# Two layers of a hybrid decoder trunk: a closing product after the last small run, and later norm transposes

## The chip, the core and the metric

The kernel runs as one program on one core of a Trainium2 chip. The metric is device time in microseconds of one execution. Three timed runs of the kernel before gave 2418.55, 2419.78 and 2422.97 us; the median, 2419.78 us, is the time that the prediction speaks of.

## The reference, cut to what matters

Each of the two layers does this, for 256 tokens and a width of 2048:

```python
u = rms_norm(x, norm_w) * (1.0 + scale) + shift
proj = jnp.dot(u, w_in)              # fq fk fv fg dq dk dv iq ... dg sz sxbc mg
y_fox = fox_attention(fq, fk, fv, log_f) * silu(fg)
y_dsa = dsa_attention(dq, dk, dv, iq, ik, iw) * silu(dg)
xbc = silu(causal_depthwise_conv(sxbc, conv_w, conv_b))
y = (ssd_scan(xs, dt, a, b, c) + d_skip * xs) * silu(sz)
y_ssd = rms_norm(y.reshape(B, S, 4, 512), ssd_norm)     # four groups of 512 channels
merged = g0 * dot(y_fox, w_o_fox) + g1 * dot(y_dsa, w_o_dsa) + g2 * dot(y_ssd, w_o_ssd)
x = x + gate * jnp.dot(merged, w_out)
```

The change lies in the state-space branch: in the norm of `y` over each of its four groups, and in what follows the last of them.

## The kernel before, in words

Every weight matrix streams from HBM in pieces of 128x1024 (`raw`). ScalarE casts a piece into a rounded upper half `wh` (L188), VectorE subtracts to get the lower half `wl` (L189), and TensorE multiplies three times for one product: upper by upper, lower by upper, upper by lower. One piece is called a half here. There are two loops over pieces. `tok_half` (L200 to L202) writes token-major banks, 12 matmuls of 512 columns a piece. `feat` (L233 to L235) writes feature-major banks, 24 matmuls of 256 columns a piece, and each of those 24 loads its own 128x128 weights (PEld, the weight load, in the rows).

The order of TensorE and SyncE is written out by hand: the instructions stand as the program issues them. After each piece the program calls `tick`, and a tick lets each of three lanes of side jobs take one step. The side jobs are generators: `g_qk`, `g_heads`, `g_xs`, `g_ssd`, `g_norm` and so on; they hold the small products (transposes against `ident`, attention and scan products) that go between the big runs. `yield from self.wait(n)` lets a job sleep for n ticks, so the `LAG_...` numbers of L63 and L64 say how many pieces later a job's next small products come. A job's lane is strictly in turn.

The state-space branch goes over four groups, g = 0 to 3. For each, `ssd_conv` runs six `feat` blocks of two pieces each through the convolution, `ssd_rest` runs eight `tok_half` pieces for the gate `sz`, and the scan job `g_ssd` issues two runs of small products, each of one 512-column product (L1022, L1025) and eight products of 64 columns (L1032) for the two token halves. Then `g_norm` forms the norm: VectorE and ScalarE multiply `y` by the gate, square, take the reciprocal root and scale `y` (L1047 to L1054); the job sleeps `LAG_NORM` ticks; TensorE transposes `y` in eight 128x128 blocks (L1059); ScalarE and VectorE split the result into `ysh` and `ysl` (L1064, L1065). With a lag of 7 the transposes of groups 0 to 2 come in the middle of the next group's convolution blocks, and those of group 3 in the middle of `gate_y("dg")` (16 pieces).

After group 3 no small product is left in the layer. What follows on TensorE, called the tail here, is one unbroken run of 4752 `feat` matmuls: the rest of `dg`, the three branch outputs with their merge gates, and the output projection. Layer 0's tail ends at the norm of layer 1 (L383), layer 1's at the end of the program.

Small products write banks of the pool `mx` (four buffers, `pbank`), big ones banks of `mm` (four buffers).

Of the kernel before, what the change touches and what calls it, by code (L numbers as in the profile page):

```python
# [60 lines left out]
AHEAD, EARLY = 1, (1,)  # L61

LAG_RMS, LAG_SM, LAG_PV, LAG_SSD = (6, 6), (3, 3), (1, 1), 3  # L63
LAG_NORM, LAG_SMALL, LAG_TOPK, LAG_DQ = (7, 7), (8, 8), (6, 6), (7, 7)  # L64
PER_TICK = 2


# [4 lines left out]
class Net:  # L72
# [968 lines left out]
    def g_norm(self, l, g, gates, y, sp, S):  # L1041

        nc, par = self.nc, self.pr[l]
        ss = self.st([P, 2], "yss")
        for c in range(2):
            t = gates[c]
            nc.vector.tensor_mul(y[:, c, :], y[:, c, :], t)  # L1047
            nc.scalar.activation(t, y[:, c, :], AF.Square, accum_out=ss[:, c:c + 1])
        rs = self.st([P, 2], "yrs")
        self.rsqrt(rs, ss, 1.0 / 2048, EPS, "ny")  # L1050
        rh = self.st([P, 2], "yrh")
        nc.vector.tensor_scalar(rh, rs, 0.5, None, op0=OP.mult)
        for c in range(2):
            nc.vector.tensor_scalar(y[:, c, :], y[:, c, :], rh[:, c:c + 1], None, op0=OP.mult)  # L1054
        yield from self.wait(LAG_NORM[self.l])
        banks = [self.pbank() for _ in range(2)]
        for i in range(4):
            for c in range(2):
                nc.tensor.transpose(banks[i // 2][:, i % 2 * SEQ + c * P:i % 2 * SEQ + c * P + P], y[:, c, i * P:i * P + P], self.ident)  # L1059
        for i in range(4):  # L1060
            f = 4 * g + i
            pt = banks[i // 2][:, i % 2 * SEQ:i % 2 * SEQ + SEQ]
            col = par[:, COLS["ssd_norm"].start + f:COLS["ssd_norm"].start + f + 1]
            nc.scalar.activation(S.ysh[:, f, :], pt, AF.Copy, scale=col)  # L1064
            nc.vector.scalar_tensor_tensor(S.ysl[:, f, :], pt, col, S.ysh.bitcast(F32)[:, f, :], op0=OP.mult, op1=OP.subtract)  # L1065
        yield
# [67 lines left out]
```

## Time and profile before

| what | value |
|---|---|
| median of three timed runs | 2419.78 us |
| the profiled execution's own time | 2399.32 us |
| its span, first to last instruction | 2397.4 us |
| PE busy | 2353.6 us, 98% |
| DVE busy | 1740.4 us, 73% |
| ACT busy | 1198.1 us, 50% |
| mean granted TensorE clock | 0.997 |

The profiled execution was 20.46 us shorter than the median of the timed ones. PE is busy nearly throughout, and matmuls overlap in the records, so busy time does not tell how fast TensorE works. What tells it is the distance from one matmul's start to the next, or the number of matmuls in a stretch: `x4414` behind a busy time is that number, with the two that had begun before the stretch among them.

### The profile page before, as it was taken

The page shows a single profiled execution, that of the slowest core. Times are in us where ns is not written, and L with a number is a line of the kernel's source. Part 1 is how long each engine was busy: PE and PEld are TensorE (multiplying, and loading weights), DVE is VectorE, ACT ScalarE, POOL GpSimd, SP SyncE. Part 2 cuts the span into 40 slices and gives each one's busy share as a digit, 9 for nine tenths or more (in the row PEclk, how much of TensorE's full clock was granted, in tenths as well). Part 3 has the DMA queues.
Part 4 walks back from the last instruction along what each step waited for, and adds up shares of the span by engine and source line. Part 5 has one row for each costly group of instructions (what it writes and reads, how often), then busy time and mean ns, then how long its engine had stood idle before and what let it go on. Part 6 is the DMA issues. An engine that isn't in the chain of part 4 may idle for free.

```text
span 2397.4 us, 43544 instructions
## 1 busy us (share of the span) xinstructions
PE 2353.6 (98%) x17192; PEld 2196.6 (92%) x17192; DVE 1740.4 (73%) x3105; ACT 1198.1 (50%) x1916; POOL 3.5 (0%) x19
## 2 busy tenths in 40 slices
PE   6999999999999999999999999999999999999999
PEld 4778889989899999999978877999999999999999
DVE  8899979778986677777765668777787655566554
ACT  3535666756454444444445555566564444444442
POOL 0000000000000000000000000000000000000000
PEclk9999999999999999999999999999999999999999
DMA  9998434567778888888855544555666666666564
GB/s 333 337 324 307 158 124 145 192 203 243 236 263 272 275 272 273 274 272 288 300 167 185 185 131 147 179 178 192 185 217 211 223 221 228 223 223 212 186 220 141
DMA packets 149919, 536.23 MB, mean 224 GB/s; under 512 B 16913, under 2 KB 17489, under 8 KB 149713
## 3 DMA queue, kind: packets, MB, share of 16 engines
q1 hardware_dynamic: 142274, 516.61, 64.9%
q10 hardware_dynamic: 7440, 16.85, 2.2%
q8 instruction: 134, 2.20, 0.4%
q14 instruction: 71, 0.58, 0.1%
HBM read 529.13 MB, written 4.26 MB: 222 GB/s over the span
## 4 chain that ended last, share of the span: by engine, by line
PE 91%; DVE 6%; ACT 1%; DMA 1%; issue 1%; SPq 0%; DVEq 0%
PE pm L233 20%; PE pm L234 20%; PE pm L235 20%; PE pm L200 8%; PE pm L202 8%; PE pm L201 8%; DVE raw L249 2%; DVE wl L189 2%; PE px L1032 1%; PE px L496 1%; DMA dec<-rows 1%; PE px L630 1%; ACT wh L188 0%; PE px L622 0%; PE held L202 0%
## 5 line engine op out<-in xcount | busy, mean ns | idle before, releaser
L188 ACT CAST wh<-raw 128x1024 fp32r<-128x1024 f32 x788 | 826.7, 1051 | 954.2 <-PE pm L234 494.8
L189 DVE TENSOR_TENSOR wl<-raw,wh 128x1024 fp32r<-128x1024 f32 x788 | 961.5, 1221 | 410.1 <-PE pm L235 176.7
L233 PE MATMUL pm<-uh,wh 128*128 128x256 f32 x2848 | 798.1, 280 | 0.0
L235 PE MATMUL pm<-uh,wl 128*128 128x256 f32 x2848 | 791.5, 278 | 0.2 <-DVE wl L189 0.2
L234 PE MATMUL pm<-ul,wh 128*128 128x256 f32 x2848 | 791.3, 278 | 0.0
L233 PEld LDWEIGHTS pm<-uh,wh 128*128 128x128 f32 x2848 | 538.9, 189 | 2.2 <-issue 2.0
L234 PEld LDWEIGHTS pm<-ul,wh 128*128 128x128 f32 x2848 | 535.1, 188 | 0.2
L235 PEld LDWEIGHTS pm<-uh,wl 128*128 128x128 f32 x2848 | 534.6, 188 | 0.4 <-DVE wl L189 0.4
L202 PE MATMUL pm<-wl,uh 128*128 128x512 f32 x896 | 351.8, 393 | 8.5 <-DVE wl L189 8.5
L200 PE MATMUL pm<-wh,uh 128*128 128x512 f32 x896 | 355.7, 397 | 1.1 <-ACT uh L399 1.1
L201 PE MATMUL pm<-wh,ul 128*128 128x512 f32 x896 | 350.5, 391 | 0.0
L249 DVE SCALAR_TENSOR_TENSOR raw<-raw,crep 128x1024 f32<-128x1024 f32 x192 | 232.9, 1217 | 0.0
L202 PEld LDWEIGHTS pm<-wl,uh 128*128 128x128 f32 x896 | 169.1, 189 | 47.4 <-DVE wl L189 11.7
L200 PEld LDWEIGHTS pm<-wh,uh 128*128 128x128 f32 x896 | 169.3, 189 | 37.7 <-issue 2.7
L201 PEld LDWEIGHTS pm<-wh,ul 128*128 128x128 f32 x896 | 169.3, 189 | 34.2 <-DVE ul L400 0.2
L235 PE MATMUL pm<-yh,wl 128*128 128x256 f32 x512 | 142.6, 279 | 0.0
L233 PE MATMUL pm<-yh,wh 128*128 128x256 f32 x512 | 142.6, 279 | 0.0
L234 PE MATMUL pm<-yl,wh 128*128 128x256 f32 x512 | 142.6, 279 | 0.0
L235 PE MATMUL pm<-ysh,wl 128*128 128x256 f32 x512 | 142.6, 279 | 0.0
L234 PE MATMUL pm<-ml,wh 128*128 128x256 f32 x512 | 142.6, 279 | 0.0
L233 PE MATMUL pm<-ysh,wh 128*128 128x256 f32 x512 | 142.6, 278 | 0.0
L234 PE MATMUL pm<-ysl,wh 128*128 128x256 f32 x512 | 142.6, 278 | 0.0
(313 smaller groups left out, 2787.2 us busy)
## 6 DMA issues: line engine op xcount, KB each, us to landing
raw<-w_ts SPq DMA_DIRECT2D x352, 512.0 KB, 4.2
raw<-w_tm SPq DMA_DIRECT2D x240, 512.0 KB, 3.6
raw<-w_ada SPq DMA_DIRECT2D x192, 512.0 KB, 4.6
raw<-w_od SPq DMA_DIRECT2D x192, 512.0 KB, 4.3
dec<-rows ACTq DMA_DIRECT2D x32, 256.0 KB, 4.2
raw<-w_sm SPq DMA_DIRECT2D x4, 512.0 KB, 4.7
xr<-xT ACTq DMA_DIRECT2D x4, 512.0 KB, 7.4
x<-xn ACTq DMA_DIRECT2D x4, 512.0 KB, 4.6
```

Source lines behind the costliest of these rows:

```text
L188: self.nc.scalar.copy(h, src)
L189: return self.nc.vector.tensor_sub(l, src, h.bitcast(F32))
L200: mm(ps, lhsT=ah, rhs=bh, start=start, stop=False)
L201: mm(ps, lhsT=al, rhs=bh, start=False, stop=False)
L202: mm(ps, lhsT=ah, rhs=bl, start=False, stop=stop)
L233: mm(ps, lhsT=h[:, c], rhs=ah[:, k, :], start=k == 0, stop=False)
L234: mm(ps, lhsT=h[:, c], rhs=al[:, k, :], start=False, stop=False)
L235: mm(ps, lhsT=l[:, c], rhs=ah[:, k, :], start=False, stop=k == nk - 1)
L249: self.in_turn(nc.vector.scalar_tensor_tensor(r, r, 0.5, self.crep[:, n % 2 * 1024:n % 2 * 1024 + 1024], op0=OP.mult, op1=OP.mult, accum_o ...
L496: nc.tensor.transpose(ps[:, j * SEQ + th * P:j * SEQ + th * P + P], t[:, th, c0 + j * P:c0 + j * P + P], self.ident)
L630: nc.tensor.matmul(po[:, :SEQ], lhsT=v[:, 0], rhs=pT[:, :SEQ], start=True, stop=False)
L1032: nc.tensor.matmul(pd[:, c * 256 + o % 256:c * 256 + o % 256 + 64], lhsT=decs[k][:, i, c, :], rhs=xd[:, c, o:o + 64], start=True, stop=True)
```

## The change

Two edits. `LAG_NORM` goes from 7 to 9 in both layers, and behind the transposes of group 3 a matmul is issued whose result nobody reads: `ones` by 64 columns of `ones`, f32, into a fresh bank of `mx`.

```diff
-LAG_NORM, LAG_SMALL, LAG_TOPK, LAG_DQ = (7, 7), (8, 8), (6, 6), (7, 7)
+LAG_NORM, LAG_SMALL, LAG_TOPK, LAG_DQ = (9, 9), (8, 8), (6, 6), (7, 7)
 ...
         for i in range(4):
             for c in range(2):
                 nc.tensor.transpose(banks[i // 2][:, i % 2 * SEQ + c * P:i % 2 * SEQ + c * P + P], y[:, c, i * P:i * P + P], self.ident)
+        if g == 3:
+
+            nc.tensor.matmul(self.pbank("idle")[:, :64], lhsT=self.ones, rhs=self.ones[:, :64], start=True, stop=True)
         for i in range(4):
             f = 4 * g + i
```

On TensorE nothing else changes place: without the eight transposes of each group and the two new matmuls, its order is the same. On PE, in layer 0, where group 1's convolution runs, this goes out (`pm` is a big bank, `px` a small one, `uh` and `ul` the halves of the layer's input):

```order
 L234 MATMUL pm<-ul,wh 128x256
 L235 MATMUL pm<-uh,wl 128x256
-L1059 MATMUL px<-ident,y 128x128 x8
 L233 MATMUL pm<-uh,wh 128x256
 L234 MATMUL pm<-ul,wh 128x256
```

and two pieces further on, where the convolution's last piece ends and the gate's first `tok_half` begins, also on PE, this comes in:

```order
 L234 MATMUL pm<-ul,wh 128x256
 L235 MATMUL pm<-uh,wl 128x256
+L1059 MATMUL px<-ident,y 128x128 x8
 L200 MATMUL pm<-wh,uh 128x512
 L201 MATMUL pm<-wh,ul 128x512
```

So group 0's transposes moved past 48 `feat` matmuls and the run of L984, L987 and L991 between them; groups 1 and 2, and layer 1, move alike. The start of layer 1's tail on PE before:

```order
L234 MATMUL pm<-ul,wh 128x256
L235 MATMUL pm<-uh,wl 128x256
L1059 MATMUL px<-ident,y 128x128 x8
L233 MATMUL pm<-uh,wh 128x256
L234 MATMUL pm<-ul,wh 128x256
```

and now:

```order
L234 MATMUL pm<-ul,wh 128x256
L235 MATMUL pm<-uh,wl 128x256
L1059 MATMUL px<-ident,y 128x128 x8
L1062 MATMUL idle<-ones 128x64
L233 MATMUL pm<-uh,wh 128x256
L234 MATMUL pm<-ul,wh 128x256
```

The transposes stand 48 matmuls later, inside `dg` as before, and a product of 64 columns now stands between them and the tail; layer 0's tail starts alike. On ACT and DVE the instructions are the same in number; L1064 and L1065 (L1067 and L1068 in the changed file) follow their transposes by the same two pieces. No DMA changes place on SP.

## Rows read from the trace of the kernel before

**Rows 1.** The page: TensorE's busy time, and the granted clock in 40 slices.

```profile
PE 2353.6 (98%) x17192; PEld 2196.6 (92%) x17192; DVE 1740.4 (73%) x3105; ACT 1198.1 (50%) x1916; POOL 3.5 (0%) x19
...
PEclk9999999999999999999999999999999999999999
```

**Rows 2.** Busy time and instructions by stretch: layer 0's tail twice, layer 1's once.

```profile
core 0: us, PE busy (x) PEld busy (x) DVE busy (x) ACT busy (x) POOL busy (x), PEclk, DMA share, GB/s
668.00:695.00 27.00, 27.00 (x232) 27.00 (x231) 23.21 (x37) 15.94 (x22) 0.00 (x0) 1.00 0.71 228
700.00:1200.00 500.00, 500.00 (x4414) 500.00 (x4414) 357.88 (x514) 221.70 (x261) 0.00 (x0) 1.00 0.83 279
1840.00:2340.00 500.00, 500.00 (x4247) 500.00 (x4247) 289.54 (x360) 215.02 (x248) 0.00 (x0) 1.00 0.67 217
```

**Rows 3.** Instructions in order of time: start, duration (us); PE where layer 1's tail begins.

```profile
1833.43 1.03 PE L1059 MATMUL px<-ident,y 128*128 128x128 f32 x8
1834.22 0.36 PE L233 MATMUL pm<-uh,wh 128*128 128x256 f32 x1
```

**Rows 4.** In order of time: PE in layer 0's tail, around 696 us.

```profile
695.91 0.28 PE L234 MATMUL pm<-ul,wh 128*128 128x256 f32 x1
696.03 0.30 PE L235 MATMUL pm<-uh,wl 128*128 128x256 f32 x1
696.17 0.28 PE L233 MATMUL pm<-uh,wh 128*128 128x256 f32 x1
```

**Rows 5.** In order of time: a run of 64-column products, and the 48 matmuls behind it.

```profile
443.76 1.90 PE L1032 MATMUL px<-xd,dec 128*128 128x64 f32 x16
445.47 0.36 PE L233 MATMUL pm<-uh,wh 128*128 128x256 f32 x1
...
451.00 0.59 PE L1025 MATMUL px<-xe,CT 128*128 128x512 f32 x1
```

**Rows 6.** By stretch, columns as in Rows 2: two of the eight long runs behind 64-column products.

```profile
455.00:475.00 20.00, 20.00 (x179) 20.00 (x178) 17.52 (x38) 14.73 (x29) 0.00 (x0) 1.00 0.55 179
...
1813.00:1833.00 20.00, 20.00 (x179) 20.00 (x178) 17.02 (x34) 9.46 (x14) 0.00 (x0) 1.00 0.57 192
```

**Rows 7.** In order of time: eight transposes, the 24 matmuls behind them, twice.

```profile
539.83 0.98 PE L1059 MATMUL px<-ident,y 128*128 128x128 f32 x7 [1.91 <-DVE y L1054]
540.57 0.37 PE L233 MATMUL pm<-uh,wh 128*128 128x256 f32 x1
...
543.39 0.27 PE L984 MATMUL px<-ident,BT 128*128 128x128 f32 x1
...
1771.21 1.03 PE L1059 MATMUL px<-ident,y 128*128 128x128 f32 x8
1772.01 0.36 PE L233 MATMUL pm<-uh,wh 128*128 128x256 f32 x1
...
1774.92 0.27 PE L984 MATMUL px<-ident,BT 128*128 128x128 f32 x1
```

**Rows 8.** Who waited for whom on PE, whole program: us in total, times, longest.

```profile
PE px L1059 <- DVE y L1054: 3.9, 2, 2.0
```

**Rows 9.** In order of time: the two waiting transposes, and the scaling of `y`.

```profile
537.64 0.27 PE L1059 MATMUL px<-ident,y 128*128 128x128 f32 x1
...
539.29 0.47 DVE L1054 TENSOR_SCALAR y<-y,yrh 128x512 f32<-128x512 f32 x1
...
602.19 0.33 PE L1059 MATMUL px<-ident,y 128*128 128x128 f32 x1
604.50 0.98 PE L1059 MATMUL px<-ident,y 128*128 128x128 f32 x7 [1.98 <-DVE y L1054]
605.23 0.36 PE L233 MATMUL pm<-uh,wh 128*128 128x256 f32 x1
```

**Rows 10.** In order of time: transposes ahead of a `tok_half` piece.

```profile
1787.19 0.47 PE L200 MATMUL pm<-wh,uh 128*128 128x512 f32 x1
1787.51 0.39 PE L201 MATMUL pm<-wh,ul 128*128 128x512 f32 x1
```

## The prediction

> **What bounds the kernel now.** I read the page first: TensorE (PE) is busy for 98% of the span, at a granted clock of nine tenths or more in every slice [rows 1]. So waits can give little, and the question is how fast the matmuls follow each other. For that I read the table by stretches, since it counts instructions. In the two tails, where the same `feat` matmul of 256 columns runs without a break, the counts differ [rows 2]. Layer 0 from 700 to 1200 us has 4414 matmuls; without the two that had begun before, that is 500 / 4412 = 113.3 ns from start to start. Layer 1 from 1840 to 2340 us has 4247, that is 500 / 4245 = 117.8 ns. The clock is 1.00 (2.4 GHz) in both, the instructions are the same, and layer 0 moves more by DMA (279 GB/s against 217), so neither the clock nor the memory explains the slower one. From 668 to 695 us layer 0's tail was slow as well: 27 / 230 = 117.4 ns. There are two paces, fast and slow, 4.46 ns apart, and a tail keeps the one it has: layer 1's stayed slow for 4752 matmuls, layer 0's went over at 696 us, at one matmul that came 0.14 us before the next and not 0.12 [rows 4], and then stayed fast.
>
> Next I looked at what stands ahead of each `feat` run in order of time. Behind the sixteen runs that end on 64-column products the pace is fast. One short one: 48 matmuls from 445.47 to 451.00, of which the first takes 0.09 more than its pace, so (5.53 - 0.09) / 48 = 113 ns [rows 5]; there are eight of these. Of the eight long ones, every stretch of 20 us holds 179 starts (20 / 177 = 113.0 ns; the slow pace would give 172) [rows 6], of which the first and the last stand there. Behind the eight runs of L1059, which are transposes alone, the pace is slow seven times: both tails [rows 2, 3] and five of six short stretches, which take 2.91 us for 24 matmuls where the one fast one takes 2.82 [rows 7]. So what ends a run of small products goes with the pace behind it, and the one before a tail decides over 4752 matmuls.
>
> Last, the waits. PE waits twice for the scaled `y` at L1059, 1.91 and 1.98 us [rows 7, 8, 9], both in layer 0.
>
> **The closing product.** It puts a 64-column f32 product between the eight transposes and each tail, the same kind of ending as the sixteen of L1032: a full 128x128 load of f32 weights, 64 columns, then L233. If it works as they do, both tails run fast from the start.
>
> Layer 1: 4752 x 4.46 ns = 21.2 us less.
>
> Layer 0, in the profiled execution: only the stretch from 667 to 696 us was slow, some 29 us, or 29 / 0.1178 = 246 matmuls, so 246 x 4.46 ns = 1.1 us less. The profiled execution took 2399.32 us, and the timed ones 2419.78: 20.46 more. Had layer 0's tail stayed slow to its end, (4752 - 246) x 4.46 ns = 20.1 us would have been added. I take this as the reason for the gap: nothing broke the slow pace in the timed runs. So against the timed median layer 0 gives 21.2 us, too.
>
> Between the ends, nothing and 42.4 us for both tails, I take 42.4. It is nearest to the rows: sixteen of sixteen endings on 64 columns were fast. What keeps it from being sure is that each of those runs had eight such products at its end, never a single one behind transposes.
>
> The product itself: the eight of an L1032 run stand in the trace as sixteen matmuls, two for each f32 product, and take (445.47 - 443.76) / 8 = 0.21 us each [rows 5]. Below, nothing can be gained by issuing it. Above, its bank was last used four banks earlier, by the product of L1025, which VectorE read before it formed this group's norm; so it should not wait; my upper end is the 0.80 us that eight transposes take without a wait [rows 7], should it stop the flow. I take 0.2 each, or +0.4 us for both.
>
> **The later transposes.** In the two places with a wait, PE takes from the first transpose to the next L233 540.57 - 537.64 = 2.93 us and 605.23 - 602.19 = 3.04 us, where it takes 0.80 without a wait (1771.21 to 1772.01) [rows 7, 9]. That is 2.13 + 2.24 = 4.4 us lost. In the new place PE comes 48 matmuls and a small run later, over 5.4 us. `y` was ready at 539.29 + 0.47 = 539.76 [rows 9], 2.1 us after PE came. So 3.3 us are to spare, and I cost the wait at nothing left: -4.4 us. If VectorE fell behind by more than that, PE would wait again, with the gate's first `tok_half` queued behind; the ends are -4.4 and 0. No other wait of PE stands between 430 and 1200 us in the waits, so I see nothing that is late next. ScalarE's and VectorE's split of the transposes (L1064, L1065) moves by the same two pieces, to where the gate begins; it is read only in the third branch's projections, far behind.
>
> The other costs are small. The five short slow stretches go (their 24 matmuls now run on from the convolution): 5 x 0.09 = -0.5 us. In place of that a `tok_half` starts six times behind transposes, with a first step of 0.32 us [rows 10] against 0.23 within a piece (half a slow step for 512 columns, 2 x 113 ns): +0.5 us. Sum 0.
>
> **Sum.** Against the profiled execution: 2399.32 - 21.2 - 1.1 + 0.4 - 4.4 = 2373.0 us. Against the median of the timed runs: 2419.78 - 42.4 + 0.4 - 4.4 = 2373.4 us. The two agree, as they should if the gap between them was layer 0's pace. I forecast 2373 us.
>
> **Rivals.**
>
> *The closing product sets nothing.* For it: one fast stretch behind transposes alone [rows 7] and the change of pace in mid-run [rows 4] show that the last product is not the whole story; it may be the rhythm of eight equal products that brings the fast pace. Against it: sixteen of sixteen. Then only the waits go: 2419.78 - 4.4 + 0.4 = 2415.8 us, a gain of 0.17%.
> The Trainium skill, in "TensorE: Matmul & The Clock Gate" (section "Back-to-back issue gap"), speaks for this rival: the spacing is set by the load and the matmul, pipelined through a window of 64 instructions, with N / 2.4 + 2.5 ns for one matmul alone. By that an unread product has no effect 64 instructions later, and the estimate for 256 columns is 109 ns whatever came before. The trace does not agree: two paces, 113.3 and 117.8 ns, each held over more than 4000 matmuls.
>
> *One tail only.* Either the product works in one layer, or the 20 us between the profiled and the timed executions have another cause and layer 0's tail was fast in both. Both give one tail's worth: 2419.78 - 21.2 - 4.4 = about 2394 us. For the second reading: the trace shows one execution alone, and its layer 0 did run fast. Against it: 20.1 us worked out from the pace and 20.46 measured.
>
> *The closing product brings the slow pace.* This is the other side. If layer 0's tail is fast in the timed runs, and the new product's weight load puts the tail into the slow rhythm and nothing breaks it at 696 us, layer 0 pays 20.1 us and layer 1 stays as it is: 2419.78 + 20.1 - 4.0 = 2436 us. It decides as soon as more than 4.0 us / 4.46 ns = 900 matmuls that ran fast become slow. Against it stand the same sixteen endings, and the 20.46 us.
>
> **How the numbers follow.** Chances: the forecast 0.70, one tail 0.13, nothing set 0.13, the slow side 0.04. For the forecast alone, with the waits' gain between 2 and 5 us and a few tenths for the products, the range is 2369 to 2377. The range for 8 in 10 takes in the one-tail case: 2367 to 2397 us, which leaves out the last two with 0.17. A measurement of this kernel can tell about 0.2%, or 4.8 us, from no change. The first two cases are faster by more. The third, at 4.0 us, lies just inside, and I split it: 0.05 faster, 0.07 same, 0.01 slower. Together 0.88 faster, 0.07 same, 0.05 slower.
>
> **What the profile of the changed kernel would show.** Right: both tails with 4414 or so matmuls in 500 us (113.3 ns), from their first microseconds on; no wait for `y` at L1059; the profiled execution within a few us of the timed ones. Wrong: a tail with 4247 in 500 us though a 64-column product stands ahead of it, which would refute that the ending sets the pace; or a wait at L1059 or L1062, in which case the lag has only moved it. If both tails are fast in the profile and the time is nonetheless near 2394 us, the 20.46 us were not layer 0's pace.

## The result and the profile after

The changed kernel takes 2393.52 us (median of 2391.74, 2393.52 and 2394.08), the kernel before 2419.78. The ratio is 0.9887, with a 95% interval of 0.9865 to 0.9910. That is 26.3 us less where 46.4 were forecast. The profiled execution of after took 2393.52 us itself, 5.8 less than the profiled one of before (2399.32). So the two kernels differ by 5.8 us when one looks at profiles and by 26.3 us when one looks at medians. Most of what follows is about that difference.

First the page of after, its busy times and the granted clock, which answer to [rows 1]:

```profile
PE 2352.6 (98%) x17196; PEld 2195.8 (92%) x17196; DVE 1740.6 (73%) x3105; ACT 1198.0 (50%) x1916; POOL 3.5 (0%) x19
...
PEclk9999999999999999999999999999999999999999
```

The page hardly tells the kernels apart: four matmuls more (two f32 products of two matmuls each) and 1.0 us of busy time less. As before, it is the count of matmuls in a stretch that says something. Here are the stretches of after that answer to [rows 2], columns as there:

```profile
670.00:690.00 20.00, 20.00 (x172) 20.00 (x172) 17.08 (x26) 12.73 (x16) 0.00 (x0) 1.00 0.66 209
700.00:1200.00 500.00, 500.00 (x4414) 500.00 (x4413) 356.76 (x510) 221.79 (x262) 0.00 (x0) 1.00 0.82 278
1840.00:2340.00 500.00, 500.00 (x4247) 500.00 (x4247) 289.24 (x359) 215.25 (x247) 0.00 (x0) 1.00 0.67 217
```

Layer 0's tail begins slow (172 in 20 us; the fast pace gives 179), and is fast from 700 us on. Layer 1's tail has 4247 matmuls in 500 us, the same number as before. Both tails now stand behind a 64-column product, and both begin slow all the same. This is what the prediction named as its refutation.

TensorE in order of time (start, duration, operation) shows why the waits went and where layer 0's pace changed:

```profile
544.17 1.03 PE L1059 MATMUL px<-ident,y 128*128 128x128 f32 x8
544.96 0.48 PE L200 MATMUL pm<-wh,uh 128*128 128x512 f32 x1
...
691.38 0.31 PE L235 MATMUL pm<-uh,wl 128*128 128x256 f32 x1
691.53 0.28 PE L233 MATMUL pm<-uh,wh 128*128 128x256 f32 x1
...
1833.20 1.03 PE L1059 MATMUL px<-ident,y 128*128 128x128 f32 x8
1834.07 0.33 PE L1062 MATMUL idle<-ones 128*128 128x64 f32 x2
1834.21 0.36 PE L233 MATMUL pm<-uh,wh 128*128 128x256 f32 x1
1834.42 0.28 PE L234 MATMUL pm<-ul,wh 128*128 128x256 f32 x1
```

The moved transposes of 544 us run through in 0.79 us without a wait, where they took 2.93 before [rows 7, 9]; no row of TensorE's waits names L1059 any more [rows 8]. At 691.38 stands the counterpart of [rows 4]: one matmul that comes 0.15 us before the next and not 0.12, at the third matmul of a group, the first to read `wl`. The closing product itself costs what was worked out: from the first transpose to L233 it is 1834.21 - 1833.20 = 1.01 us, where [rows 3] have 0.79, so 0.22 more.

What holds that one matmul back can be read on VectorE and on the weight loads (PEld), in order of time in the same execution:

```profile
684.01 2.35 DVE L189 TENSOR_TENSOR yl<-yf,yh 128x1024 fp32r<-128x1024 f32 x2
686.28 2.35 DVE L189 TENSOR_TENSOR yl<-yd,yh 128x1024 fp32r<-128x1024 f32 x2
...
690.03 2.35 DVE L189 TENSOR_TENSOR wl<-raw,wh 128x1024 fp32r<-128x1024 f32 x2
...
691.15 0.19 PEld L234 LDWEIGHTS pm<-ul,wh 128*128 128x128 f32 x1
691.30 0.19 PEld L235 LDWEIGHTS pm<-uh,wl 128*128 128x128 f32 x1
```

Four splits of the branch outputs (`yl`) stand ahead of the weight's. The first of the two `wl` is ready at about 690.03 + 1.22 = 691.25 us, and the load that reads it as weights starts at 691.30, 0.15 us behind the load before it, where the slow pace has 0.12. So TensorE waits some 0.03 us, too little for a row in the view of waits, and goes on at the other pace. The trace of before has the same wait at [rows 4].

### The profile page after: what moved, and what is told of

Read it like the earlier page. It is cut to its first block, busy times and chain, and to the rows that moved or that the text cites. A ratio compares the mean times of both kernels' runs of the same rounds, so it can differ in the third digit from the quotient of the medians.

```text
span 2391.7 us, 43556 instructions
## 1 busy us (share of the span) xinstructions
PE 2352.6 (98%) x17196; PEld 2195.8 (92%) x17196; DVE 1740.6 (73%) x3105; ACT 1198.0 (50%) x1916; POOL 3.5 (0%) x19
## 4 chain that ended last, share of the span: by engine, by line
PE 93%; DVE 6%; issue 1%; ACT 0%; DMA 0%; SPq 0%; DVEq 0%; ACTq 0%
PE pm L233 21%; PE pm L235 21%; PE pm L234 21%; PE pm L200 8%; PE pm L202 8%; PE pm L201 8%; DVE wl L189 2%; DVE raw L249 2%; PE px L1032 1%; PE px L496 1%; PE px L630 1%; PE held L202 0%; PE px L622 0%; PE held L200 0%; PE held L201 0%
## 5 line engine op out<-in xcount | busy, mean ns | idle before, releaser
L233 PE MATMUL pm<-uh,wh 128*128 128x256 f32 x2848 | 797.3, 280 | 0.0
L233 PEld LDWEIGHTS pm<-uh,wh 128*128 128x128 f32 x2848 | 534.9, 188 | 2.2 <-issue 2.0
L233 PE MATMUL pm<-yh,wh 128*128 128x256 f32 x512 | 142.6, 279 | 0.0
L233 PE MATMUL pm<-ysh,wh 128*128 128x256 f32 x512 | 142.6, 278 | 0.0
L233 PE MATMUL pm<-mh,wh 128*128 128x256 f32 x512 | 142.6, 278 | 0.0
```

Of the source, the lines that this page charges most:

```text
L233: mm(ps, lhsT=h[:, c], rhs=ah[:, k, :], start=k == 0, stop=False)
```

## Experiments

The theory after the result: the 64-column product does nothing to the pace, the later transposes are worth some 6 us, and the other 20 us are layer 0's tail, which was slow to its end in the three timed runs of before and turns fast at the wait for `wl` in other executions. Rivals: the rhythm of eight equal products is what makes the fast pace; or the edit does work, but its product is too short; or the 20 us are a difference between executions that has nothing to do with the pace. In each of three sets of runs before was timed again on the same chip; its times fell in two groups, 2397.7 to 2404.4 and 2418.2 to 2425.0 us. Where a ratio mixes these, I compare with the nearest kernel of the same set.

**Before again, and the two edits apart.** e1 is before, unchanged. e2 has only

```diff
-LAG_NORM, LAG_SMALL, LAG_TOPK, LAG_DQ = (7, 7), (8, 8), (6, 6), (7, 7)
+LAG_NORM, LAG_SMALL, LAG_TOPK, LAG_DQ = (9, 9), (8, 8), (6, 6), (7, 7)
```

and e3 has only

```diff
+        if g == 3:
+            nc.tensor.matmul(self.pbank("idle")[:, :64], lhsT=self.ones, rhs=self.ones[:, :64], start=True, stop=True)
```

> The kernel before, unchanged, to see an execution at its timed level. Theory A (layer 0's tail stayed slow in the timed runs, and the profiled execution at 2399.32 us is one in which a short wait for wl broke the slow pace): executions fall into two groups, about 2399 and 2419 us; in a profile at 2419 layer 0's tail has about 4247 matmuls in 500 us throughout, in one at 2399 about 4414. Rival B (the 20 us have another cause): a profiled execution at 2419 us still shows 4414 matmuls in 500 us in layer 0, or executions spread evenly.

> Only the norm lag of 9; no closing product. Theory A (the product sets no pace; the gain is the two waits and layer 0's tail breaking into the fast pace more reliably because of where the tail now begins): 2393 us, as with both edits, both tails slow at their start. Theory C (the product is what lets layer 0 break): layer 0's tail slow to its end in the timed runs, 2419.8 - 4.4 = 2415 us.

> Only the closing product, norm lag of 7. Theory A: the waits at L1059 are back, so 4 us above both edits if layer 0's tail breaks (2398 us), or as before (2420 us) if it does not; both tails start slow. Theory C (the product lets layer 0 break): 2398 us. The prediction's step, that the product makes both tails fast from the start, would give 2378 us.

Measured: e1 2399.89 us (2397.74 to 2403.88, ten runs), e2 2393.98 (2391.83 to 2397.21, seven), e3 2400.26 (2398.68 to 2403.95, ten); before beside them 2402.26, with one of 24 runs in the upper group. So the lag alone gives 5.9 us against e1, and 7.0 by its ratio to the runs of before beside it (0.9971, 0.9960 to 0.9982). The product alone gives +0.4, which can't be told from zero: e1 and the runs beside it are one kernel and lie 2.4 us apart. In e3 both tails begin slow, as in after:

```profile
670.00:690.00 20.00, 20.00 (x172) 20.00 (x171) 15.99 (x29) 9.89 (x14) 0.00 (x0) 1.00 0.80 264
1840.00:2340.00 500.00, 500.00 (x4248) 500.00 (x4247) 288.95 (x361) 215.35 (x248) 0.00 (x0) 1.00 0.66 217
```

The view of waits gives for e1 (us in total, times, longest), where [rows 8] had two waits:

```profile
PE px L1059 <- DVE y L1054: 4.7, 3, 2.0
```

There is a third, small one in this execution (0.85 us), so 4.4 us was a low reading of what the lag can give.

**Is the product too short?** e4 is after with 256 columns in place of 64, e7 with 128:

```diff
-nc.tensor.matmul(self.pbank("idle")[:, :64], lhsT=self.ones, rhs=self.ones[:, :64], start=True, stop=True)
+nc.tensor.matmul(self.pbank("idle")[:, :SEQ], lhsT=self.ones, rhs=self.tri, start=True, stop=True)   # e4
+nc.tensor.matmul(self.pbank("idle")[:, :P], lhsT=self.ones, rhs=self.ones, start=True, stop=True)    # e7
```

> Both edits, but the unread closing product is 256 columns wide (ones by tri, f32) and not 64. In the trace of before all runs that end on f32 products of 256 columns (L682, L721) are followed by the fast pace. Theory D (what counts is that TensorE streams a product longer than a weight load, so that the load of the first feat matmul stands behind it): both tails fast from the start, 2393.5 - 20.9 - 1.0 + 0.3 = 2372 us. Theory A (no closing product sets the pace, only a wait does): 2393 to 2394 us, layer 1's tail slow.

> Both edits, with an unread closing product of 128 columns. Theory D (the product has to outlast the weight load ahead of the tail): the two matmuls of a 128-column product are about as long as a load, so it lies at the edge; L631 with 128 columns is followed by the fast pace in the trace of before, but behind L630 with 256. Fast in both tails gives 2372 us and would mean that any f32 product over 64 columns does; slow gives 2393.6 us and puts the edge between 128 and 256.

e4 took 2374.41 us (2372.70 to 2376.66, four runs), 19.6 below e2 of the same set; its ratio to before is 0.9888 (0.9872 to 0.9905). By stretches, e4:

```profile
700.00:1200.00 500.00, 500.00 (x4414) 500.00 (x4414) 356.93 (x510) 221.93 (x261) 0.00 (x0) 1.00 0.81 278
1840.00:1860.00 20.00, 20.00 (x179) 20.00 (x178) 17.52 (x24) 12.39 (x15) 0.00 (x0) 1.00 0.66 199
1870.00:2360.00 490.00, 490.00 (x4326) 490.00 (x4326) 284.83 (x352) 213.03 (x241) 0.00 (x0) 1.00 0.68 221
```

And TensorE in order of time where layer 1's tail begins, to be held against after's rows at 1833 us:

```profile
1833.59 1.03 PE L1059 MATMUL px<-ident,y 128*128 128x128 f32 x8
1834.46 0.60 PE L1062 MATMUL idle<-tri,ones 128*128 128x256 f32 x2
1834.71 0.47 PE L233 MATMUL pm<-uh,wh 128*128 128x256 f32 x1
1835.02 0.28 PE L234 MATMUL pm<-ul,wh 128*128 128x256 f32 x1
```

Layer 1's tail has 179 in its first 20 us and 4326 in 490 us: 490 / 4324 = 113.3 ns, the fast pace. The transposes ahead, the operands of the tail and the code around it are the same as in after; only the product's columns differ (and the operand they are read from).

Three of e7's four runs took 2372.01, 2372.77 and 2373.30 us, and the profiled one 2391.68. Its stretches tell why:

```profile
668.00:688.00 20.00, 20.00 (x178) 20.00 (x178) 17.61 (x27) 12.75 (x17) 0.00 (x0) 1.00 0.65 215
700.00:1200.00 500.00, 500.00 (x4248) 500.00 (x4247) 346.00 (x494) 213.90 (x251) 0.00 (x0) 1.00 0.80 269
1850.00:2350.00 500.00, 500.00 (x4415) 500.00 (x4414) 299.61 (x374) 224.03 (x259) 0.00 (x0) 1.00 0.69 226
```

Both tails begin fast, so 128 columns do as well. But layer 0's turned slow in this execution, at the same wait for `wl` where after's turned fast:

```profile
688.91 0.28 PE L234 MATMUL pm<-ul,wh 128*128 128x256 f32 x1
689.27 0.39 PE L235 MATMUL pm<-uh,wl 128*128 128x256 f32 x1
```

The two starts are 0.36 us apart here, so TensorE waits 0.25 us; the tail came fast and is earlier at this place. e4 and e12 have the same 0.36 and stay fast. One more place can be compared, in every profiled execution: 74 matmuls into a run of 192 in layer 1 (1505.95 us in after), which is fast until there, the starts stand 0.44 us apart, so TensorE waits 0.33 us for `wl`. Behind it ten of the fourteen stay fast and four turn slow (e1, e4, e6, e7). By stretch, after and then e4:

```profile
1508.00:1518.00 10.00, 10.00 (x91) 10.00 (x90) 6.62 (x10) 4.30 (x5) 0.00 (x0) 1.00 0.78 272
1508.00:1518.00 10.00, 10.00 (x87) 10.00 (x87) 6.22 (x10) 3.91 (x5) 0.00 (x0) 1.00 0.81 264
```

So a wait at the fast pace can leave that pace or end it. At the slow pace a wait was followed by the fast one in all ten places that were profiled (layer 0 of before, after, e1, e2, e3, e5, e6, e10 and e11, layer 1 of e10); a wait with the slow pace on both sides was not seen.

**Or the rhythm of eight?** e6 is after with eight 64-column products, as an L1032 run has them:

```diff
+            ib = self.pbank("idle")
+            for i in range(8):
+                nc.tensor.matmul(ib[:, i * 64:i * 64 + 64], lhsT=self.ones, rhs=self.ones[:, :64], start=True, stop=True)
```

> Both edits, but eight unread 64-column products (1.7 us a layer) and not one. Theory E (the rhythm of several equal f32 products is what the sixteen L1032 runs have and a single product lacks): both tails fast, 2393.5 - 21.9 + 3.0 = 2375 us. Theory D (what counts is a last product longer than a load of weights, as in the one of 256 columns): both tails start slow, 2393.5 + 3.0 = 2396.5 us.

The ten runs fell in two groups, five at 2397.5 to 2398.3 us and five at 2416.2 to 2418.8. In the profiled one, of the lower group, TensorE's rows read like those of [rows 5], but with transposes ahead of them:

```profile
1836.42 1.03 PE L1059 MATMUL px<-ident,y 128*128 128x128 f32 x8
1837.29 1.90 PE L1064 MATMUL idle<-ones 128*128 128x64 f32 x16
1838.99 0.36 PE L233 MATMUL pm<-uh,wh 128*128 128x256 f32 x1
```

The next 20 us of this execution by stretch:

```profile
1840.00:1860.00 20.00, 20.00 (x172) 20.00 (x171) 14.60 (x20) 11.92 (x14) 0.00 (x0) 1.00 0.53 175
```

172 is the slow pace, so the rhythm theory falls. A run that looks the same, down to the 0.36 us of the first L233, is followed by the fast pace in the sixteen places of before and by the slow one here.

**Take layer 0's wait away.** e8 is before, with the split of `yd` in layer 0 moved from the tail's first weight to its later ones, so that VectorE has `wl` ready earlier:

```diff
-                    self.split(yh[:, a:a + 4], yl[:, a:a + 4], src[:, a:a + 4])
+                    if l or not n:
+                        self.split(yh[:, a:a + 4], yl[:, a:a + 4], src[:, a:a + 4])
...
+                if l == 0 and br == 0 and c in (8, 12):
+                    a = c % 8
+                    with self.first():
+                        self.split(yhl[1][0][:, a:a + 4], yhl[1][1][:, a:a + 4], yd[:, a:a + 4])
```

> The kernel before, but layer 0 splits yd into yh and yl eight and twelve channel blocks into the first branch and not ahead of it, so that VectorE is 2.3 us earlier with the wl that TensorE waits for at 696 us. Theory A (that wait of a tenth of a us is what makes layer 0's tail fast): the wait is gone and with it the fast pace; layer 0's tail has about 4247 matmuls in 500 us and the time is 2399.9 + 20 = 2420 us, the level of the three timed runs of before. Rival (layer 0's tail turns fast for another reason): 4414 in 500 us and 2400 us, or 2399.7 without the wait.

It took 2422.34 us (2418.14 to 2424.30): all ten runs lie in the upper group, while before beside it had 15 of 25 in the lower and 10 in the upper. Layer 0's tail by stretch:

```profile
700.00:1200.00 500.00, 500.00 (x4248) 500.00 (x4247) 347.35 (x493) 213.07 (x250) 0.00 (x0) 1.00 0.80 269
```

Here `wl` is ready at 697.60 + 1.22 = 698.82 us and read 2.74 us later:

```profile
697.60 1.22 DVE L189 TENSOR_TENSOR wl<-raw,wh 128x1024 fp32r<-128x1024 f32 x1
```

With no wait nothing ends the slow pace. The upper group is thus what a slow layer 0 costs: 22.5 us above the lower one's median in this set (2399.88), where 20.1 were worked out from the pace. That before's upper runs have the same cause is an inference from this: no execution of before in the upper group was profiled, so it isn't known either whether the wait leaves layer 0 slow there or, at 0.03 us, does not come at all.

**Make such a wait in layer 1.** e5 and e10 are after with two, and three, further writes of the last `yl` piece on VectorE ahead of `wl`:

```diff
+                if l == 1 and n == 1:
+                    for _ in range(2):          # e10: 3
+                        nc.vector.tensor_sub(yl[:, 4:8], src[:, 4:8], yh[:, 4:8].bitcast(F32))
```

> Both edits, and in layer 1 VectorE computes the last piece of yl twice more (2.3 us of work with the same result), ahead of a wl that TensorE found ready only 1.6 us before its use. TensorE then has to wait some 0.7 us for wl about 24 us into layer 1's tail, as it waits shortly in layer 0's. Theory A (a wait of TensorE inside a slow run is what turns it fast): layer 1's tail slow until there, then 4414 matmuls in 500 us; 2393.5 - (4704 - 240) x 4.46 ns + 0.7 = 2374 us, faster by doing more. Rival (only what stands ahead of a run, or which layer it is, sets its pace): layer 1's tail slow to its end, 2393.5 + 0.7 = 2394 us.

> Both edits with the 64-column product, and in layer 1 three more repeats of the last piece of yl on VectorE, since two left wl 0.70 us before its use and made no wait. With three, wl ends some 0.45 us after TensorE comes for it, 26 us into layer 1's tail, which is slow there. Theory A2 (a wait deals the pace anew): layer 1's tail fast from there in some or all executions, 2393.5 + 0.5 - 20.5 = 2373 to 2374 us where it is; a mix of 2374 and 2394 would show the dealing. Rival (layer 1's pace is not open to a wait): 2394 us throughout.

e5 took 2395.52 us (2391.89 to 2397.77) and tested nothing: two repeats left the nearest `wl` ready 0.70 us early, TensorE did not wait, and the tail stayed slow. e10 took 2373.61, 2375.65 and 2376.10 us, and once 2397.26 (median 2375.87, ratio to before 0.9844, 0.9788 to 0.9900). In the profiled run of 2375.65 us, by stretch, ahead of the wait and behind it:

```profile
1840.00:1860.00 20.00, 20.00 (x172) 20.00 (x171) 16.44 (x23) 12.14 (x15) 0.00 (x0) 1.00 0.59 183
1870.00:2360.00 490.00, 490.00 (x4326) 490.00 (x4326) 285.80 (x352) 213.80 (x243) 0.00 (x0) 1.00 0.68 223
```

And between them TensorE in order of time:

```profile
1864.53 0.28 PE L234 MATMUL pm<-ul,wh 128*128 128x256 f32 x1
1864.65 0.33 PE L235 MATMUL pm<-uh,wl 128*128 128x256 f32 x1
1864.82 0.28 PE L233 MATMUL pm<-uh,wh 128*128 128x256 f32 x1
```

The wait is shorter than expected (0.05 us and not 0.45) and comes one piece later, 28.6 us into the tail. Some 3.5 us of useless work on VectorE, and this wait on the engine that bounds the kernel, make it about 20 us faster. This is the clearest evidence that a wait sets the pace: the rest of the kernel is after's, and e5 has two of the three repeats, no wait, and a slow tail. The one run at 2397.26 was not profiled; one slow tail, in either layer, would give it.

**A version that is better than both.** e9 has the 256-column product of e4, the later transposes, and e8's later split, so that nothing should deal a fast tail anew. e11 is after again, e12 is e4's product without the lag:

```diff
-LAG_NORM, LAG_SMALL, LAG_TOPK, LAG_DQ = (9, 9), (8, 8), (6, 6), (7, 7)    # e4
+LAG_NORM, LAG_SMALL, LAG_TOPK, LAG_DQ = (7, 7), (8, 8), (6, 6), (7, 7)    # e12
```

> Both edits with the closing product of 256 columns, and layer 0's split of yd moved eight and twelve channel blocks into the first branch, so that TensorE's short wait for wl early in layer 0's tail is gone. Theory A2 (a product of 256 columns starts both tails fast, and a short wait deals the pace anew, either way): with nothing left to deal it anew, every execution is fast in both tails, 2373 us and within 2 us of each other. Rival (the wait is what keeps layer 0 fast): layer 0 slow, 2394 us.

> The kernel with both edits, unchanged, against many executions of the kernel before on one chip. Theory A2 (the 64-column product sets nothing, the lag takes the two waits away, and layer 0's pace after its wait is dealt in both kernels): executions near 2394 us, with the kernel before near 2400 us in its lower group, so 6 us apart where both have layer 0 fast; some executions of either 20 us higher. Prediction's step (the product sets the pace): no upper group in this kernel.

> The closing product of 256 columns alone, with the norm lag of 7. Theory A2 (the two edits add up: the pace from the wide product, the waits from the lag): both tails fast from the start, and the waits at L1059 back: 2374.4 + 6 = 2380 us. Rival (the start of the tail two pieces later has a part in the pace): a tail slow, 2394 to 2400 us.

e9 took 2373.04 us (2372.64 to 2374.09, four runs), e11 2394.29 (2391.78 to 2396.35), e12 2381.49 (2378.48 to 2383.34). Before beside them had six of seven runs in the upper group, median 2420.82; e9's ratio to it is 0.9814 (0.9770 to 0.9858). e9 is 21.3 us below after (e11), and its runs lie within 1.5 us. e4's four runs, with the wait, were all fast as well, so four runs do not show what the later split is worth. Its tails by stretch:

```profile
700.00:1190.00 490.00, 490.00 (x4326) 490.00 (x4325) 350.90 (x501) 217.78 (x256) 0.00 (x0) 1.00 0.82 279
1870.00:2360.00 490.00, 490.00 (x4326) 490.00 (x4325) 285.14 (x351) 212.88 (x241) 0.00 (x0) 1.00 0.68 221
```

e12 against e4 (of another set) puts the lag at 7.1 us, beside 5.9 and 7.0 above.

## Why the prediction came out as it did

The measured time lies at the value of the second rival, "one tail only", and 20 us off the forecast of 2373. It is inside the range because the range took that rival in, and that is luck: the product works in neither layer, and the 20 us between the executions were layer 0's pace after all, so neither reading of that rival is what happened.

*The two paces, and that they are worth 21 us a tail: right.* e4 against e2 is 19.6 us, nearly all of it layer 1, and e8 against the lower runs of before 22.5 for layer 0, where 20.1 were worked out.

*"The closing product": wrong, and it is the main step.* "If it works as they do, both tails run fast from the start": it does not. The fault lies in "sixteen of sixteen endings on 64 columns were fast". This was a correlation without a case that differs only in the ending, and the prediction did not look at what stands ahead of the sixteen. TensorE in the trace of before, in order of time, at one of each of their two kinds (eight each):

```profile
442.91 1.02 PE L1022 MATMUL px<-xe,Bt 128*128 128x512 f32 x2
...
451.00 1.02 PE L1025 MATMUL px<-xe,CT 128*128 128x512 f32 x2
451.86 1.89 PE L1032 MATMUL px<-xd,dec 128*128 128x64 f32 x16
```

Each has an f32 product of 512 columns right ahead of it, where the closing product has transposes; and e6 shows that eight 64-column products behind transposes leave the pace slow. Nor does it speak of the other runs that end on transposes. One of them stands 3 us behind a run of L1059, in order of time:

```profile
1646.79 1.03 PE L1059 MATMUL px<-ident,y 128*128 128x128 f32 x8
1647.58 0.36 PE L233 MATMUL pm<-uh,wh 128*128 128x256 f32 x1
...
1650.49 0.27 PE L984 MATMUL px<-ident,BT 128*128 128x128 f32 x1
1650.60 0.61 PE L987 MATMUL px<-CT,BT 128*128 128x128 f32 x4
1651.05 0.60 PE L991 MATMUL px<-ident,xc 128*128 128x128 f32 x4
1651.40 0.37 PE L233 MATMUL pm<-uh,wh 128*128 128x256 f32 x1
...
1654.22 0.40 PE L200 MATMUL pm<-wh,uh 128*128 128x512 f32 x1
```

Behind the eight transposes alone, 24 matmuls take 2.91 us, the slow pace; behind the run of L984, L987 and L991, which ends on transposes too but has f32 products of 128 columns (L987) ahead of them, they take 2.82, the fast one. Counted through the trace of before: `feat` runs right behind an f32 product of 128 or 256 columns are fast in 26 of 26 places, behind such a product with transposes after it in 14 of 15, behind a wider one with 64 columns after it in 16 of 16, and behind transposes alone in 5 of 14. A reading that fits these rows and runs: an f32 product of 128 columns or more makes the pace fast, 64 columns and transposes behind it mostly leave it so, and transposes alone mostly do not keep it. The first part is shown by an edit for 128 and 256 (e7, e4); the others are only counted, and were not tested by themselves, for instance with a 256-column product ahead of the 64-column one.

*The rival "the closing product sets nothing": its mechanism was right, its time was not.* It subtracted 4.4 us from 2419.78. From the window of 64 instructions in the section "Back-to-back issue gap" of the Trainium skill's page "TensorE: Matmul & The Clock Gate" the prediction read that an unread product has no effect so far behind it; the page itself does not say that. The runs agree with this reading for 64 columns and not for 128 and 256: there the unread product makes over 4700 matmuls faster.

*The 20.46 us between the profiled and the timed executions: read rightly, and then used wrongly.* They were layer 0's tail, as the prediction said, as far as e8 and the pace let one infer. But it concluded that "nothing broke the slow pace in the timed runs" and counted 21.2 us as the closing product's to give. It had the place in [rows 4] and put no cause to it: what breaks the pace there is the wait for `wl`, which is in the traces of both kernels. Of the 26.3 us, about 6 are the later transposes (e2). The other 20 or so are, by inference, that the three timed runs of before had a slow layer 0 to the end and those of after had not. Against e1's median, in the lower group (2399.89, another set), after's 2393.52 is a ratio of 0.997.

*The later transposes: right, and a little small.* -4.4 was worked out from two waits; 5.9 to 7.1 were measured. The prediction put two things at nothing: the third wait, and the clock behind the waits. Before and then e1, by stretch, behind the second place of [rows 9]:

```profile
606.00:612.00 6.00, 6.00 (x54) 6.00 (x53) 5.96 (x16) 3.53 (x9) 0.00 (x0) 1.00 0.76 234
606.00:612.00 6.00, 5.02 (x24) 5.03 (x25) 5.32 (x13) 2.62 (x5) 0.00 (x0) 0.51 0.76 238
```

In e1 the granted clock falls to 0.51 there, close to the lower of its two levels (1.2 GHz), after TensorE had stood still for 0.85 and then 1.98 us. From TensorE's coming to these transposes to its next L1032 e1 takes 36.4 us and before 32.8. e8 shows such a fall too; e3, e12 and before, also with the lag of 7, do not, and none of the nine traces with a lag of 9 has a granted clock under 0.97 in any 5 us between 300 and 660 us. At the first place `y` is scaled by 539.84 us, 4.3 before the transposes start at 544.17, where 3.3 were expected.

*The product's own cost: right* (0.22 us each in the trace of after, where 0.2 were expected; the times of e3 and e1 can't tell it from zero).

Open: why after's layer 0 never stayed slow. With a lag of 9 and either no product or one of 64 columns, all 24 timed runs lie at the level of a fast layer 0 (after 3, e2 7, e5 10, e11 4), while before lay in the upper group in 3 of 3, 1 of 24, 10 of 25 and 6 of 7 of the runs beside them. If e5 were dealt like the 25 runs beside it, ten in a row in the lower group would have a chance of 0.6 to the tenth power, or 0.6%. So chance is a poor explanation, and the change may well earn some or all of the 20 us; no run shows by what. The lag does not suffice, since e6 has it too, with eight products, and lay in its upper group in 5 of 10. The wait has the same length in the profiles of before and after. Also open is why 128 columns differ from 64. In order of time, L233's first step is 0.21 us behind 64 columns and behind 128, and 0.31 behind 256, so the first step does not tell the pace.

## What to carry to other kernels

Where one engine is 98% busy, count its instructions per stretch before and after, since the busy share does not show a pace that is 4% off. A pattern seen at every place of one kind ("sixteen of sixteen") is a cause only if the places differ in nothing else, so look for what stands ahead of them, too. When the profiled execution and the timed median lie 20 us apart, find out which of the two levels each kernel is at before any of it is put down to the change.

## What the runs showed that was not expected

The same pairs of weight load and 256-column matmul, at a granted clock of 1.00 (2.4 GHz), run at 113.3 or at 117.8 ns from start to start, and keep that over 4700 matmuls and 530 us. It goes with the small products ahead: behind eight transposes, or these with 64 columns after them, the tails began slow in every trace; with an f32 product of 128 or 256 columns after them, fast.

A wait of 0.02 to 0.33 us of TensorE amid such matmuls can change the pace: the slow pace became the fast one in all ten profiled places (after at 691 us, e10 at 1864), and the fast pace stayed or became the slow one (e7 at 689). So taking a wait away can cost 22 us (e8), and adding useless work off the path can gain 20 (e10).
